# Activation and weight buffers 32 bytes further apart in SBUF

## The chip, the cores and the metric

The kernel runs on one core of a Trainium2 chip. The metric is the device time of one execution in microseconds (us). The kernel before took 1582.41 us as the median of three runs (1581.74 to 1587.0 us).

## The reference

Two layers of a transformer-like trunk run over 256 context tokens and 256 latent tokens of width 1024, batch 1, all in float32. Cut to the parts that matter here:

```
for i in range(2):
    mod, modc = silu(c) @ w_mod[i] + b_mod[i], silu(c_ctx) @ w_mod[i] + b_mod[i]
    h  = rms_norm(x,  norm1_g[i]) * (1 + mod[1])  + mod[0]
    hc = rms_norm(xc, norm1_g[i]) * (1 + modc[1]) + modc[0]
    parts = split(h @ w_in[i]), split(hc @ w_in[i])     # spatial-gating MLP, attention, Mamba-2
    x  = x + mod[2] * (concat(gmlp, attention, ssd) @ w_out[i])
    hf = rms_norm(x, norm2_g[i]) * (1 + mod[4]) + mod[3]
    # layer 0: one SwiGLU of width 2816 for all 512 tokens
    # layer 1: top 2 of 8 SwiGLU experts for the 256 latent tokens
    x  = x + mod[5] * f
```

The three head groups (a chunked spatial-gating MLP, windowed attention with a sink, a two-way Mamba-2 scan) lie between the input and the output projection; the change does not touch them.

## The kernel before

Everything lies transposed: the 1024 features are 8 blocks of 128 partitions, the 512 tokens run along a partition's bytes. `phase_a` computes layer 0 and the mixer of layer 1, `experts` the eight experts of layer 1.

**Weights.** Every weight is fetched as a piece of 128 partitions by 2048 floats (1024 KB, 8192 bytes in each partition) into a tile `wraw` (`Weights._load`; the DMA is issued by SyncE, L240). `wraw` tiles are slots of a ring: four in the pool `w`, and for the experts five more in the pool `mk` and three in the pool `mp`. `advance` fetches whenever a slot is free, and with twelve slots it runs far ahead in the expert stage.

**Two-term float32.** Most projections run as three matmuls in the type float32r. A weight piece is split by `Weights._split` into `whi` (a copy by ScalarE, L275) and `wlo` = `wraw` − `whi` (by VectorE, L276), each in two halves; the normed activations are split in `norm` into `ahi` (L520) and `alo` (L523 or L525), sixteen tiles `act` of 128 by 512. `project` then adds `ahi`·`whi`, `alo`·`whi` and `ahi`·`wlo` for each block of 128 features (all matmuls are recorded at L374, the line of the helper `mm`). In `project` the weight slice is the stationary operand and the activation tile the moving one. In `gmlp_v`, which writes `gvp`, it is the other way round: 128 tokens of `ahi` are stationary, and 264 columns of the weight tile move, from column 264·k in step k. Small experts multiply straight from `wraw` in plain float32.

**Order.** What stands in which order on an engine comes from the program's generators and from `Order`, a clock of estimated costs; no size or address of a tile enters it. SyncE's queue holds the weight DMAs in the order of the plan; a fetch waits for the last reader of the tile that had the slot.

**Where tiles lie.** A pool's tiles stand one after the other in each partition, and the pools one after the other. In the built program every one of the large tiles begins 224 bytes into a 256-byte row of SBUF (its start address modulo 256 is 224): `wraw`, `whi`, `wlo`, `ahi`, `alo`, the general tiles `g` (which hold `mhi`, `mlo`, `xT` and most others), and the slots of `mk` and `mp`. The reason is that each of these tiles has a multiple of 256 bytes (8448 or 8192 for weights, 2048 for the others). The one large tile that begins elsewhere is the second of the two `xp` tiles of the convolution, at 0 (a tile of 2080 bytes); the first is at 224.

Of the kernel before, what the change touches and what calls it, by code (L numbers as in the profile page):

```python
# [9 lines left out]
F32 = mybir.dt.float32  # L10
F32R = mybir.dt.float32r
# [7 lines left out]
P = 128  # L19
# [12 lines left out]
CONV_K = 5  # L32
GD = 264
WW = KB * GD

CONSTS = {}
NCONST = 0
# [172 lines left out]
def until(cond):  # L210
    while not cond():
        yield 0.5


class Weights:
# [14 lines left out]
    def _load(self):  # L230
        i = self.i_load
        _, src, width, _ = self.items[i]
        net = self.net
        if isinstance(src, tuple):
            _, p, c, j = src
            src = net.d["moe"][0, c, j] if p == NE - 1 else net.d["moe"][bass.ds(net.expert(p), 1), c, j].rearrange("e p f -> p (e f)")
        pool, bufs = self.ring[self.at_ring]
        self.at_ring = (self.at_ring + 1) % len(self.ring)
        t = pool.tile([P, WW if pool is net.wp else 2048], F32, tag="raw", name="wraw", bufs=bufs)
        net.nc.sync.dma_start(t[:, :width], src)  # L240
        self.raw[i] = t
        self.at[i] = net.o.clk
        self.queue = self.land[i] = max(self.queue + net.PIECE, net.o.clk + net.LANDS)
        self.raw_live += 1
        self.i_load += 1
# [7 lines left out]
    def _split(self, halves=2):  # L253
        i = self.i_split
        _, _, width, split = self.items[i]
        if not split:
            self.i_split += 1
            return
        net = self.net
        nc = net.nc  # L260
        t = self.raw[i]
        if not self.half:
            n = self.nsplit % self.nhi
            self.nsplit += 1
            pool, bufs = (net.wp, 2) if n < 2 else (net.mp, self.nhi - 2)
            ww = WW if pool is net.wp else 2048
            hi = pool.tile([P, ww], F32R, tag="hi", name="whi", bufs=bufs)
            lo = pool.tile([P, ww], F32R, tag="lo", name="wlo", bufs=bufs)
            self.hl[i] = (hi, lo, t) if split > 1 else (hi, lo)
            self.hi_live += 1  # L270
        hi, lo = self.hl[i][:2]
        n = net.NS
        for h in range(self.half, min(n, self.half + halves)):
            cs = slice(width // n * h, width // n * (h + 1))
            nc.scalar.activation(hi[:, cs], t[:, cs], AF.Copy)  # L275
            nc.vector.tensor_tensor(lo[:, cs], t[:, cs], hi[:, cs].bitcast(F32), op=ALU.subtract)  # L276
            self.splits = max(self.splits, net.o.clk, self.land[i]) + net.SPLIT
            self.ready.setdefault(i, self.splits + net.SPLIT)
        self.half += halves
        if self.half < n:  # L280
            return
        self.half = 0
        self.i_split += 1
        if split == 1:
            self.raw_live -= 1
            del self.raw[i]
# [54 lines left out]
class Net:  # L341
# [136 lines left out]
    def norm(self, l, which, xready, halves=False):  # L478

        nc = self.nc  # L480
        ps = self.pp.tile([P, 512], F32, tag="n", name="ssq", bufs=1)
        self.act = None

        def sums(k, a, b):

            sq0, sq = self.G(name="sq"), self.G(name="sq")
            nc.scalar.activation(sq0[:, a:b], self.xT[k - 1][:, a:b], AF.Square)
            nc.vector.tensor_tensor(sq[:, a:b], self.xT[k][:, a:b], self.xT[k][:, a:b], op=ALU.mult)
            nc.gpsimd.tensor_tensor(sq0[:, a:b], sq0[:, a:b], sq[:, a:b], op=ALU.add)
            return sq0  # L490

        last = KB - 2 if halves else KB
        for k in range(last):
            yield from until(lambda: all((k, s) in xready for s in range(2)))
            if k % 2:
                sq = sums(k, 0, T)
                if halves:
                    if k > 1:
                        nc.gpsimd.tensor_tensor(sq, sq, tot, op=ALU.add)
                    tot = sq  # L500
                else:
                    yield 2.5
                    self.mm(ps, self.c("ones"), sq, k == 1, k == KB - 1)
        a = 24 * which
        m = self.modT[l]
        sc = None
        mods_in = lambda: all((l, j) in self.mods_done for j in range(6 * which, 6 * which + 4))
        his, los = [], []
        for k in range(KB):
            his.append(self.gb.tile([P, 512], F32R, tag="act", name="ahi"))  # L510
            los.append(self.gb.tile([P, 512], F32R, tag="act", name="alo"))

        def apply(ks, s, r):
            cs = slice(256 * s, 256 * s + 256)
            for k in ks:
                u = self.G(name="nu")
                nc.vector.scalar_tensor_tensor(u[:, cs], self.xT[k][:, cs], sc[:, k, s:s + 1], r, op0=ALU.mult, op1=ALU.mult)
                sh = m[:, a + k, s:s + 1]
                hi, lo = his[k][:, cs], los[k][:, cs]
                nc.scalar.activation(hi, u[:, cs], AF.Identity, bias=sh)  # L520
                if k % 2:
                    nc.scalar.activation(u[:, cs], u[:, cs], AF.Identity, bias=sh)
                    nc.gpsimd.tensor_tensor(lo, u[:, cs], hi.bitcast(F32), op=ALU.subtract)  # L523
                else:
                    nc.vector.scalar_tensor_tensor(lo, u[:, cs], sh, hi.bitcast(F32), op0=ALU.add, op1=ALU.subtract)  # L525

        if halves:
            for s in (1, 0):
                yield from until(lambda: all((k, s) in xready for k in (KB - 2, KB - 1)))
                c0 = 256 * s  # L530
                sq = sums(KB - 1, c0, c0 + 256)
                if s == 1:
                    yield 1.8
                    self.mm(ps[:, c0:c0 + 256], self.c("ones"), tot[:, c0:c0 + 256], True, False)
                    self.mm(ps[:, c0:c0 + 256], self.c("ones"), sq[:, c0:c0 + 256], False, True)
                    r1 = self.rsqrt(ps[:, c0:c0 + 256], 1.0 / D, 256)[:, :256]
                    if mods_in():
                        sc = self.scales(l, which)
            if sc is None:
                yield from until(mods_in)  # L540
                sc = self.scales(l, which)
            apply(range(self.H1), 1, r1)
            yield 0.5
            self.mm(ps[:, :256], self.c("ones"), tot[:, :256], True, False)
            self.mm(ps[:, :256], self.c("ones"), sq[:, :256], False, True)
            r0 = self.rsqrt(ps[:, :256], 1.0 / D, 256)[:, :256]
            apply(range(self.H1, KB), 1, r1)
            apply(range(KB), 0, r0)
            yield self.H2
            self.act = (his, los)  # L550
            return
        r = self.rsqrt(ps, 1.0 / D, T)
        yield from until(mods_in)
        sc = self.scales(l, which)
        for k in range(KB):
            for s in range(2):
                apply((k,), s, r[:, 256 * s:256 * s + 256])
        yield 6.0
        self.act = (his, los)
# [644 lines left out]
    def plan(self):  # L1204
# [6 lines left out]
        def win(l):  # L1211
            n = self.mods_seq()[1] + self.MODS_C if l else 4
            for x in self.ORDER[l]:
# [3 lines left out]
                elif x == "g":  # L1217
                    it.append((("wgd", l), d["wgd"][l], WW, True))
                else:
# [583 lines left out]
    def overflow_of(self, e, past=0):  # L1803
# [28 lines left out]
        for c in range(NCH):  # L1832
            w = []
            for i in range(3):
                t_ = self.wp.tile([P, WW], F32, tag="raw", name="wraw", bufs=self.nraw)
                nc.sync.dma_start(t_[:, 0:2048], self.d["moe"][e, c, i].rearrange("e p f -> p (e f)"))
                w.append(t_)
            ps = self.bank("ogu")
# [106 lines left out]
```

## Time and profile before

| | |
|---|---|
| median of three runs | 1582.41 us |
| the profiled execution | 1583.83 us |
| its span, first to last instruction | 1582.1 us |
| mean granted TensorE clock | 0.978 |
| PE busy | 1500.2 us (95%) |
| DVE busy | 821.2 us (52%) |
| ACT busy | 666.7 us (42%) |
| DMA queue 1 | 392.03 MB, 62.2% of 16 engines' span |

PE is TensorE's matmuls, PEld its weight loads, DVE VectorE, ACT ScalarE, POOL GpSimd, SP SyncE. The span has two stages: up to about 890 us the phase before the experts, with DMA engines busy a third of the time; from about 900 us to 1545 us the experts, where the DMA engines are busy nearly without a break. A matmul's start is recorded; its end is modelled, so the distance from start to start of successive matmuls tells their rate better than the length shown.

### The profile page before, as it was taken

Reading aid. Unit: us, or ns where it says so; the run is one execution under the profiler, and the core shown is the slowest. Engines: PE = TensorE matmul, PEld = TensorE weight load, DVE = VectorE, ACT = ScalarE, POOL = GpSimd, SP = SyncE. Lnnn points to the kernel's source line nnn. Section 1 sums busy time; section 2 is a strip of 40 time slices with the busy share of each in tenths; the row PEclk is TensorE's granted clock in tenths of the full one; section 3 lists DMA queues with packets and bytes.
Section 4 is the critical chain, followed back from the end, with each engine's and each line's share of the span. In section 5 each row is a group of like instructions: output and inputs, shape, how many; then the busy total and the mean of one; then the engine's idle time right before and its main releaser. Section 6 shows DMA issues by size and latency. Waiting matters only on the chain. (4 is left out here: it accounts for less than half of the span.)

```text
span 1582.1 us, 23498 instructions
## 1 busy us (share of the span) xinstructions
PE 1500.2 (95%) x9302; PEld 1081.1 (68%) x9303; DVE 821.2 (52%) x1481; ACT 666.7 (42%) x1189; POOL 102.6 (6%) x135
## 2 busy tenths in 40 slices
PE   5999998899999999999999899999999999999997
PEld 1766675787887787878757776666566666656654
DVE  2687568543232333378774344544465444654545
ACT  3566644443222312266455354444343443433441
POOL 1200123210000000030300000000000000000000
PEclk9999999999999999999999899999999999999998
DMA  9422055333323323333164499999998999999994
GB/s 372 152 106 107 28 211 202 133 133 112 129 91 149 133 107 113 112 141 142 56 267 181 152 418 419 419 419 420 418 390 358 371 413 417 419 402 407 419 420 158
DMA packets 57715, 396.10 MB, mean 250 GB/s; under 512 B 6528, under 2 KB 8576, under 8 KB 10496
## 3 DMA queue, kind: packets, MB, share of 16 engines
q1 hardware_dynamic: 56016, 392.03, 62.2%
q10 hardware_dynamic: 1584, 2.52, 0.4%
q8 instruction: 75, 1.23, 0.3%
q14 instruction: 40, 0.33, 0.1%
HBM read 393.47 MB, written 1.05 MB: 249 GB/s over the span
## 5 line engine op out<-in xcount | busy, mean ns | idle before, releaser
L276 DVE TENSOR_TENSOR wlo<-wraw,whi 128x1024 fp32r<-128x1024 f32 (+2 forms) x318 | 377.0, 1222 | 161.2 <-ACT whi L275 155.9
L275 ACT ACTIVATE whi<-wraw 128x1024 fp32r<-128x1024 f32 (+2 forms) x318 | 320.0, 1047 | 148.5 <-PE fd L374 57.9
L374 PE MATMUL gu<-whi,xw 128*128 128x512 f32 x528 | 169.1, 401 | 4.2 <-ACT whi L275 4.2
L374 PE MATMUL gu<-wraw,xs 128*64 128x256 f32 (+1 forms) x1760 | 166.2, 386 | 0.5 <-ACT xs L1484 0.5
L374 PEld LDWEIGHTS gu<-wraw,xs 128*64 128x64 f32 (+1 forms) x1760 | 94.4, 127 | 64.3 <-issue 14.6
L374 PEld LDWEIGHTS gu<-whi,xw 128*128 128x128 f32 x528 | 96.9, 190 | 24.5 <-ACT whi L275 6.1
L374 PE MATMUL gu<-wlo,xw 128*128 128x512 f32 x264 | 104.9, 397 | 3.5 <-DVE wlo L276 3.5
L1162 DVE TENSOR_TENSOR fsil<-fsil,fu 128x512 f32<-128x512 f32 x22 | 15.1, 688 | 153.5 <-PE fu L374 118.2
L374 PE MATMUL pys<-wraw,silx 128*32 128x256 f32 (+1 forms) x616 | 87.6, 480 | 6.8 <-DVE y L1770 4.1
L425 ACT ACTIVATE fsil<-fg 128x512 f32<-128x512 f32 x22 | 13.1, 598 | 174.3 <-PE fg L374 174.3
L1573 ACT ACTIVATE mid<-gu 128x256 f32<-128x256 f32 x55 | 21.0, 382 | 137.1 <-PE gu L374 137.1
L374 PE MATMUL fg<-ahi,whi 128*128 128x512 f32 (+1 forms) x192 | 72.3, 377 | 0.0
L374 PE MATMUL fg<-alo,whi 128*128 128x512 f32 (+1 forms) x192 | 71.6, 373 | 0.2 <-POOL alo L523 0.2
L374 PE MATMUL fg<-ahi,wlo 128*128 128x512 f32 (+1 forms) x192 | 71.4, 372 | 0.0
L374 PE MATMUL fu<-alo,whi 128*128 128x512 f32 (+1 forms) x192 | 71.4, 372 | 0.0
L374 PE MATMUL fu<-ahi,wlo 128*128 128x512 f32 (+1 forms) x192 | 71.3, 372 | 0.0
L374 PE MATMUL fu<-ahi,whi 128*128 128x512 f32 (+1 forms) x192 | 71.3, 372 | 0.0
L374 PE MATMUL fd<-mhi,whi 128*128 128x512 f32 (+1 forms) x188 | 70.7, 376 | 0.0
L374 PE MATMUL fd<-mlo,whi 128*128 128x512 f32 (+1 forms) x188 | 70.6, 375 | 0.0
L374 PE MATMUL fd<-mhi,wlo 128*128 128x512 f32 (+1 forms) x188 | 70.6, 375 | 0.0
L374 PE MATMUL modp<-wraw,csil 128*32 128x512 f32 x384 | 56.7, 628 | 12.0 <-ACT csil L425 6.9
L374 PEld LDWEIGHTS gu<-wlo,xw 128*128 128x128 f32 x264 | 49.9, 189 | 18.3 <-DVE wlo L276 7.4
(342 smaller groups left out, 2831.8 us busy)
## 6 DMA issues: line engine op xcount, KB each, us to landing
wraw<-in_moe_dram SPq DMA_DIRECT2D x264, 1024.0 KB, 12.6
wraw<-in_wmod_dram SPq DMA_DIRECT2D x48, 1024.0 KB, 6.4
wraw<-in_fgu_dram SPq DMA_DIRECT2D x22, 1024.0 KB, 4.8
wraw<-in_win_dram SPq DMA_DIRECT2D x16, 1024.0 KB, 4.9
wraw<-in_wout_dram SPq DMA_DIRECT2D x8, 1024.0 KB, 6.2
wraw<-in_fdn_dram SPq DMA_DIRECT2D x8, 1024.0 KB, 6.2
wraw<-in_fdn_dram SPq DMA_DIRECT2D x4, 768.0 KB, 4.9
wraw<-in_wgd_dram SPq DMA_DIRECT2D x2, 1056.0 KB, 4.9
```

Source lines behind the costliest of these rows:

```text
L275: nc.scalar.activation(hi[:, cs], t[:, cs], AF.Copy)
L276: nc.vector.tensor_tensor(lo[:, cs], t[:, cs], hi[:, cs].bitcast(F32), op=ALU.subtract)
L374: self.nc.tensor.matmul(out, l, r, start=start, stop=stop)
L425: self.last_act = self.nc.scalar.activation(out, in_, func, **kw)
L1162: self.nc.vector.tensor_tensor(s, s, pu, op=ALU.mult)
L1573: self.nc.scalar.activation(v, ps[:, :256], AF.Copy)
```

## The change

Three widths grow by eight floats, 32 bytes: tiles `wraw`, `whi` and `wlo` of the pool `w` (2112 to 2120 columns) and the `act` tiles (512 to 520, of which 512 are used). Nothing else is edited.

```diff
+SKEW = 8
@@ Weights._load
-        t = pool.tile([P, WW if pool is net.wp else 2048], F32, tag="raw", name="wraw", bufs=bufs)
+        t = pool.tile([P, WW + SKEW if pool is net.wp else 2048], F32, tag="raw", name="wraw", bufs=bufs)
@@ Weights._split
-            ww = WW if pool is net.wp else 2048
+            ww = WW + SKEW if pool is net.wp else 2048
             hi = pool.tile([P, ww], F32R, tag="hi", name="whi", bufs=bufs)
             lo = pool.tile([P, ww], F32R, tag="lo", name="wlo", bufs=bufs)
@@ norm
-            his.append(self.gb.tile([P, 512], F32R, tag="act", name="ahi"))
-            los.append(self.gb.tile([P, 512], F32R, tag="act", name="alo"))
+            his.append(self.gb.tile([P, 512 + SKEW], F32R, tag="act", name="ahi")[:, :512])
+            los.append(self.gb.tile([P, 512 + SKEW], F32R, tag="act", name="alo")[:, :512])
@@ overflow_of
-                t_ = self.wp.tile([P, WW], F32, tag="raw", name="wraw", bufs=self.nraw)
+                t_ = self.wp.tile([P, WW + SKEW], F32, tag="raw", name="wraw", bufs=self.nraw)
```

In the built program the start addresses modulo 256 become:

| tiles | before | after |
|---|---|---|
| `wraw`, four slots in `w` | 224 each | 224, 0, 32, 64 |
| `whi`, two tiles | 224 each | 96, 128 |
| `wlo`, two tiles | 224 each | 160, 192 |
| `act`, sixteen tiles | 224 each | 224, 0, 32, 64, 96, 128, 160, 192, twice over |
| `wraw`, five slots in `mk`, three in `mp` | 224 each | 224 each |
| `g` tiles, `xw`, `mh`, `ml`, `hr` | 224 each | 224 each |
| `xp`, two tiles | 224, 0 | 224, 0 |

The eight tiles of `w` grow by 8 · 32 = 256 bytes together, so all that stands behind them moves by one whole row and keeps its place within one. The instructions of every engine, their order, and the semaphores and values they wait for are the same in the two built programs; only addresses differ.

## Rows read from the trace of the kernel before

**Rows 1.** Page, head and part 1: busy us (share of span) xinstructions.

```profile
span 1582.1 us, 23498 instructions
...
PE 1500.2 (95%) x9302; PEld 1081.1 (68%) x9303; DVE 821.2 (52%) x1481; ACT 666.7 (42%) x1189; POOL 102.6 (6%) x135
```

**Rows 2.** Engines by stretch; its first line names the columns.

```profile
core 0: us, PE busy (x) PEld busy (x) DVE busy (x) ACT busy (x) POOL busy (x), PEclk, DMA share, GB/s
...
250.00:500.00 250.00, 242.05 (x1240) 198.45 (x1239) 110.64 (x162) 77.42 (x115) 21.22 (x18) 1.00 0.35 128
500.00:665.00 165.00, 165.00 (x747) 133.79 (x746) 55.73 (x75) 41.83 (x54) 1.29 (x1) 1.00 0.32 115
...
920.00:1100.00 180.00, 174.87 (x1156) 117.98 (x1157) 86.21 (x106) 83.83 (x136) 0.00 (x0) 0.99 1.01 419
...
1300.00:1500.00 200.00, 192.84 (x1302) 125.03 (x1301) 106.90 (x143) 84.06 (x129) 0.00 (x0) 0.98 1.01 413
```

**Rows 3.** DMA in 920 to 1100 us: queue, packets, MB, share; issues, us to landing.

```profile
q1 hardware_dynamic: 10333, 75.24, 100.9%
...
wraw<-in_moe_dram SPq DMA_DIRECT2D x74, 1024.0 KB, 16.0
```

**Rows 4.** PE in time, 512 columns, 560 to 566 us: start, length.

```profile
559.64 0.39 PE L374 MATMUL fd<-mlo,whi 128*128 128x512 f32 x1
...
565.99 0.39 PE L374 MATMUL fd<-mhi,wlo 128*128 128x512 f32 x1
```

**Rows 5.** PE in time, 256 columns, 300 to 303 us.

```profile
299.73 0.28 PE L374 MATMUL op<-ahi,wlo 128*128 128x256 f32 x1
...
300.81 0.28 PE L374 MATMUL op<-ahi,wlo 128*128 128x256 f32 x1
```

**Rows 6.** PE in time, `gvp`, 264 columns: every third matmul of 24 in a row.

```profile
717.53 0.28 PE L374 MATMUL gvp<-whi,ahi 128*128 128x264 f32 x1
...
717.89 0.29 PE L374 MATMUL gvp<-whi,ahi 128*128 128x264 f32 x1
...
718.26 0.28 PE L374 MATMUL gvp<-whi,ahi 128*128 128x264 f32 x1
...
718.62 0.28 PE L374 MATMUL gvp<-whi,ahi 128*128 128x264 f32 x1
...
718.98 0.29 PE L374 MATMUL gvp<-whi,ahi 128*128 128x264 f32 x1
...
719.35 0.28 PE L374 MATMUL gvp<-whi,ahi 128*128 128x264 f32 x1
...
719.70 0.28 PE L374 MATMUL gvp<-whi,ahi 128*128 128x264 f32 x1
...
720.06 0.28 PE L374 MATMUL gvp<-whi,ahi 128*128 128x264 f32 x1
...
720.43 0.28 PE L374 MATMUL gvp<-whi,ahi 128*128 128x264 f32 x1
```

**Rows 7.** Groups by line and shape: xcount | busy us, mean ns | idle before.

```profile
L276 DVE TENSOR_TENSOR wlo<-wraw,whi 128x1024 fp32r<-128x1024 f32 x306 | 364.4, 1227 | 160.4 <-ACT whi L275 155.2 <-PE tok L379 4.2
...
L374 PE MATMUL gu<-whi,xw 128*128 128x512 f32 x528 | 169.1, 401 | 4.2 <-ACT whi L275 4.2
...
L374 PE MATMUL fd<-mhi,whi 128*128 128x512 f32 x164 | 63.8, 389 | 0.0
...
L374 PE MATMUL fg<-alo,whi 128*128 128x512 f32 x160 | 62.4, 390 | 0.0
```

**Rows 8.** Page, part 5: VectorE at 512 elements.

```profile
L1162 DVE TENSOR_TENSOR fsil<-fsil,fu 128x512 f32<-128x512 f32 x22 | 15.1, 688 | 153.5 <-PE fu L374 118.2
```

**Rows 9.** Single lines, ns min/median/max: L276 at 94-100 us, L275 at 704-709 us, L783 everywhere.

```profile
L276 DVE TENSOR_TENSOR wlo<-wraw,whi x2: 1249/1250/1251, 96.6 to 97.9; 128x1056 fp32r<-128x1056 f32 x2
...
L275 ACT ACTIVATE whi<-wraw x2: 1071/1071/1071, 704.5 to 705.9; 128x1056 fp32r<-128x1056 f32 x2
...
L783 DVE SCALAR_TENSOR_TENSOR convacc<-xp,params,convacc x48: 479/740/752, 85.3 to 747.7; 128x512 f32<-128x512 f32 x40, 128x256 f32<-128x256 f32 x8
```

## The prediction

> **What bounds the kernel now.** The page's head and first part come first: PE is busy for 1500.2 of 1582.1 us [rows 1], but a share over the whole span hides that the kernel has two stages with different limits. The view by stretches parts them [rows 2]. From 500 to 665 us PE is busy for 165.00 of 165.00 us at granted clock 1.00, with the DMA share at 0.32: there every nanosecond that a matmul gains or loses is a nanosecond of the kernel. From 920 to 1100 us and from 1300 to 1500 us the DMA share is 1.01, at 419 and 413 GB/s. The DMA view of the first of these stretches says what this is: one queue's packets take 100.9% of the sixteen engines' time, and a fetch lands 16.0 us after its issue [rows 3]. One fetch of 1024 KB is 1.0486 MB, and at 419 GB/s it takes 2.50 us, so some six are always queued. In the expert stage the fetches set the pace, and PE, DVE and ACT only follow.
>
> So an address can matter in two ways: through the rate of PE's matmuls before 890 us, and through the rate of the fetches after it. VectorE and ScalarE are third: they limit where a split ends last before a matmul, which is seldom (4.2 us of idle PE before `gu` for `whi`, [rows 7]).
>
> **What the change does, part by part.** No instruction, DMA or wait is added, removed or moved; so nothing has to be hidden, and the sum consists of durations alone. Of the tiles only those listed as moved get another place within a 256-byte row: 4 of the 12 fetch slots have new widths and 3 of them a new place; `whi` and `wlo` of `w` all move; the `act` tiles spread over eight places. The `g` tiles, `xw` and eight fetch slots keep theirs.
>
> *Matmuls.* In `fd`, where three matmuls of 512 columns follow each other without a break, 28 intervals take 565.99 − 559.64 = 6.35 us, 226.8 ns each [rows 4]. [...] The direct test stands in the trace too. In `gvp` the moving weights of step k begin at column 264·k, 1056·k bytes, which is 32 bytes further in a row at each step, while the stationary `ahi` stays at 224 plus a multiple of 512 bytes. Three matmuls a step, eight steps, so all eight places occur. The starts are 0.36, 0.37, 0.36, 0.36, 0.37, 0.35, 0.36 and 0.37 us apart [rows 6]: 2.90 us for 24, 120.8 ns each, no step out of line by more than the 10 ns of the reading. The step in which weights and activation share a place is neither quicker nor slower. The roles of the operands are swapped against `project`, which is why this is strong but no proof. I take 0 ns for each matmul. For the ends: none of the eight places can differ by more than about 0.01 us over three matmuls, 3.3 ns for each. In `project` a piece of weights meets 8 steps, 3 terms and 2 column blocks, 48 matmuls; with 22 pieces for `fg` and `fu` and 16 for the two input projections that makes 38 · 48 = 1824, some 1800 of the 9302 PE instructions [rows 1], with both operands on moved tiles. 1800 · 3.3 ns is 5.9 us either way if every one went to one end; as the places spread over all eight, I keep half of it, ±3 us.
>
> *Splits on DVE and ACT.* L276 takes a mean of 1227 ns for 1024 elements, and the same kind of operation, there with one input in PSUM, takes 688 ns for 512 [rows 7, 8]: (1227 − 688)/512 = 1.05 ns for each further element. Two SBUF inputs at one place cost no visible extra over one. Again places already differ in the trace. The two halves of the gate piece are 1056 elements; the second begins 4224 bytes on, at place (224 + 4224) mod 256 = 96. DVE takes 1249 and 1251 ns for the two halves of one layer's piece, ACT 1071 and 1071 for the other layer's [rows 9]. The convolution reads `xp` at 224 and at 0 in turn, at four shifts each; forty operations on 512 elements and eight on 256 stay between 479 and 752 ns with a median of 740, and a second level for the second tile doesn't show [rows 9]. I take 0, with ±10 ns as the end. The 306 splits of 1024 elements at 10 ns are 3.1 us of DVE time, and DVE is busy for 55.73 of 165 us and 86.21 of 180 us [rows 2]; PE's own stream and the fetches cover them, so nothing reaches the end. Without that cover it would be the 3.1 us.
>
> *Fetches.* Here no row of mine compares two places, since every slot begins at 224; so the cost has to be bounded. Upper end: 0, the time of a fetch goes by its bytes. Lower end: it goes by the bytes from the start of the first row. A partition's 8192 bytes from place 224 span 8416 from the row's start; from 0, 32 and 64 they span 8192, 8224 and 8256, shorter by 2.7%, 2.3% and 1.9%. In the expert stage 264 fetches go round 12 slots, 22 for each, at 2.50 us. 22 · 2.50 · (0.027 + 0.023 + 0.019) = 3.8 us less. If it went by the number of rows touched (33 from 224, 32 from 0, 33 from 32 and 64), only one slot would gain, 22 · 2.50/33 = 1.7 us. A loss has no such source: no slot begins later in a row than before. In the first stage the DMA share of 0.32 to 0.35 hides any gain. I take 0: it is the value nearest to what the same layout gives today, 419 GB/s steadily.
>
> [...]
>
> The sum is 0 against the profiled execution's 1583.83 us (span 1582.1 and 1.7 around it). That execution lies 1.4 us above the median of the three runs, so the forecast is that median, 1582.4 us.
>
> **The rivals.** *A, fetches gain by their place*, the lower end above: 1582.4 − 3.8 = 1578.6 us, or 1580.7 if it goes by rows touched. For it: the expert stage is bound by fetches. Against it: only 3 of 12 slots move, and nothing in the trace shows a loss at 224. Both values lie within 0.3% (4.7 us), about what a measurement of this kernel can tell from no change.
>
> [...]
>
> *C, slower: operands at unlike places hinder each other*, which equal places avoid today because the streams run in step. [...] The price is taken from `gu<-whi,xw`, the slowest of the 512-column groups, 401 against 389 ns [rows 7], though fetches and waits may explain it: 1800 · 12 ns · 7/8 = 18.9 us, 1601.3 us. It decides as soon as a matmul costs over 4.7 us/1800 = 2.6 ns more. Against it: `gvp` again, where seven of eight pairs are unlike.
>
> *D, less is changed than it seems*: the eight tiles of `w` add up to 256 bytes, so most tiles stay where they were. This is so, whatever the places cost; it makes each of the others smaller and gives 1582.4.
>
> **How the numbers follow.** No change (with D) gets 0.80, A 0.11, B 0.05, C 0.04. A counts as within 0.3% but at its end it comes near the edge, so I give 0.02 of it to faster. Faster is 0.05 + 0.02 = 0.07; slower is C's 0.04 and 0.01 more for a run like the highest of the three; the same is what is left, 0.88. The range reaches down to A's end, 1578.5, and up to the highest of the three runs, 1587.0; it leaves out B and C.
>
> **What would show it.** In the profile after, the intervals of `fd` should again be 227 ns and those of `op` 120; the mean of `fg<-alo,whi` should stay at 390 ns and that of `fd` at 389; L276 at 1227 ns within 10; PE busy in 500 to 665 us without a gap; the DMA rate from 920 to 1100 us at 419 GB/s, within 3. [...] Any change of more than 5 us would make the prediction wrong, above all one before 890 us.

## The result

| | before | after |
|---|---|---|
| median | 1582.54 us (4 runs) | 1596.22 us (4 runs) |
| lowest to highest | 1581.74 to 1587.0 | 1593.57 to 1596.65 |
| profiled execution, its span | 1583.83, 1582.1 us | 1593.57, 1591.7 us |
| mean granted clock | 0.978 | 0.977 |

The changed kernel takes 1.0078 times as long, with an interval of 1.0061 to 1.0095: 12.3 us more (9.7 to 15.0). The forecast was no change, and the time lies outside its range. The profiled executions differ by 9.7 us, their spans by 9.6 us; where those lie can be read from the traces.

The page's head and first part, to set against [rows 1]: the same 23498 instructions, PE busy for 11.9 us longer, the span 9.6 us longer.

```profile
span 1591.7 us, 23498 instructions
...
PE 1512.1 (95%) x9302; PEld 1081.5 (68%) x9303; DVE 821.6 (52%) x1481; ACT 667.6 (42%) x1189; POOL 103.5 (7%) x135
```

Next three stretches, with the columns and the windows of [rows 2].

```profile
500.00:665.00 165.00, 165.00 (x732) 131.10 (x731) 52.25 (x70) 39.88 (x51) 0.00 (x0) 1.00 0.32 115
...
920.00:1100.00 180.00, 173.43 (x1158) 117.22 (x1157) 85.21 (x110) 85.05 (x142) 0.00 (x0) 0.99 1.01 420
1300.00:1500.00 200.00, 192.94 (x1284) 125.01 (x1285) 106.69 (x145) 84.22 (x130) 0.00 (x0) 0.98 1.00 413
```

From 500 to 665 us PE is busy without a gap at granted clock 1.00, as before, but starts 732 matmuls in the 165 us instead of 747 [rows 2]. Nothing waits more; each matmul takes longer (747/732 = 1.020). The DMA rate from 920 to 1100 us is 420 GB/s against 419. The matmuls in time show the price of one:

```profile
565.12 0.39 PE L375 MATMUL fd<-mlo,whi 128*128 128x512 f32 x1
...
571.59 0.39 PE L375 MATMUL fd<-mhi,wlo 128*128 128x512 f32 x1
...
299.07 0.28 PE L375 MATMUL op<-ahi,wlo 128*128 128x256 f32 x1
...
300.12 0.28 PE L375 MATMUL op<-ahi,wlo 128*128 128x256 f32 x1
...
724.50 0.28 PE L375 MATMUL gvp<-whi,ahi 128*128 128x264 f32 x1
...
727.42 0.28 PE L375 MATMUL gvp<-whi,ahi 128*128 128x264 f32 x1
```

The first column is the start. `fd`: 28 intervals in 6.47 us, 231.1 ns each, against 226.8 [rows 4]. `op` with 256 columns: nine in 1.05 us, 116.7 ns against 120.0 [rows 5]. `gvp` with 264: 24 in 2.92 us, 121.7 ns against 120.8 [rows 6]. So one edit makes matmuls of 512 columns slower, those of 256 columns faster, and leaves the mean of those of 264 nearly as it was. The groups by line and shape agree, and the other engines' lines stay:

```profile
L277 DVE TENSOR_TENSOR wlo<-wraw,whi 128x1024 fp32r<-128x1024 f32 x306 | 364.4, 1228 | 160.9 <-ACT whi L276 154.9 <-PE tok L380 4.4
...
L375 PE MATMUL gu<-whi,xw 128*128 128x512 f32 x528 | 171.1, 405 | 4.2 <-ACT whi L276 4.2
...
L375 PE MATMUL fd<-mhi,whi 128*128 128x512 f32 x164 | 64.9, 396 | 0.0
...
L375 PE MATMUL fg<-alo,whi 128*128 128x512 f32 x160 | 62.9, 393 | 0.0
```

Against [rows 7], `gu`, `fd` and `fg` gain 3 to 7 ns in length, the split on VectorE 1 ns.

**Where the 9.6 us lie.** First and last starts of three tiles mark the stages. Here before and then after; a row has the number, the length in ns (least/median/most) and the first and last start in us.

```profile
L374 PE MATMUL fg<-ahi,whi x192: 279/389/504, 309.1 to 649.1; 128*128 128x512 f32 x160, 128*128 128x256 f32 x32
...
L374 PE MATMUL fd<-mhi,whi x188: 277/389/390, 414.1 to 684.3; 128*128 128x512 f32 x164, 128*128 128x256 f32 x24
...
L374 PE MATMUL gu<-whi,xw x528: 387/389/775, 928.5 to 1534.3; 128*128 128x512 f32 x176
```

```profile
L375 PE MATMUL fg<-ahi,whi x192: 278/393/500, 308.8 to 655.7; 128*128 128x512 f32 x160, 128*128 128x256 f32 x32
...
L375 PE MATMUL fd<-mhi,whi x188: 274/394/404, 415.9 to 691.3; 128*128 128x512 f32 x164, 128*128 128x256 f32 x24
...
L375 PE MATMUL gu<-whi,xw x528: 387/394/775, 934.2 to 1543.8; 128*128 128x512 f32 x176
```

The SwiGLU of layer 0, first `fg` to last `fd`, takes 684.3 − 309.1 = 375.2 us before and 691.3 − 308.8 = 382.5 us after: +7.3. The experts, first `gu` to last `gu`, take 605.8 and 609.6 us: +3.8. What lies ahead of the first comes to −0.3 us, what lies between the two (244.2 and 242.9 us, the mixer of layer 1 with its many 256-column matmuls) to −1.3 us, and the tail to +0.1. 7.3 + 3.8 − 0.3 − 1.3 + 0.1 = 9.6. The lengths of the SwiGLU and of the experts, called the SwiGLU stretch and the expert stretch, are given for the experiments too. Only these two differences are clear of what varies between executions: before and in the experiments that keep the operands alike in the stretch in question (3, 5, 9, 10 and 12), the SwiGLU stretch is 375.2 to 376.6 us and the expert stretch 604.9 to 605.8, while what lies between the two is 240.8 to 244.8, so the −1.3 us there shows nothing.

### The profile page after: what moved, and what is told of

Its sections match the earlier page's. It is cut to its first block, busy times and chain, and to the rows that moved or that the text cites. A ratio compares the mean times of both kernels' runs of the same rounds, so it can differ in the third digit from the quotient of the medians.

```text
span 1591.7 us, 23498 instructions
## 1 busy us (share of the span) xinstructions
PE 1512.1 (95%) x9302; PEld 1081.5 (68%) x9303; DVE 821.6 (52%) x1481; ACT 667.6 (42%) x1189; POOL 103.5 (7%) x135
## 3 DMA queue, kind: packets, MB, share of 16 engines
HBM read 393.47 MB, written 1.05 MB: 248 GB/s over the span
## 5 line engine op out<-in xcount | busy, mean ns | idle before, releaser
L276 ACT ACTIVATE whi<-wraw 128x1024 fp32r<-128x1024 f32 (+2 forms) x318 | 320.3, 1048 | 152.2 <-PE fd L375 59.3
```

## The experiments

**How a matmul is read.** For each kernel I took the mean distance from a float32r matmul's start to the next one's where the next follows without a wait (distances of 220 to 245 ns for 512 columns, 100 to 135 ns for 256), by the tile of the first of the two. It is worked out from all such starts in the trace, in ns:

| | fd 512 | fg 512 | gu 512 | py 512 | fg 256 | op 256 |
|---|---|---|---|---|---|---|
| before | 226.7 | 227.4 | 228.9 | 227.9 | 120.0 | 119.5 |
| after | 232.1 | 231.5 | 232.7 | 232.4 | 118.3 | 117.7 |
| 1 weights' pool alone | 232.0 | 232.4 | 232.7 | 232.4 | 120.1 | 117.9 |
| 2 `act` tiles alone | 226.8 | 231.1 | 228.9 | 227.7 | 117.7 | 119.5 |
| 3 all at byte 0 | 226.7 | 227.4 | 228.2 | 227.6 | 120.0 | 119.6 |
| 4 weights' pool at 96 | 233.3 | 234.7 | 232.4 | 233.0 | 120.0 | 118.7 |
| 5 fetch tiles alone | 226.7 | 227.4 | 228.8 | 227.8 | 120.0 | 119.5 |
| 6 `wlo` alone at 96 | 231.1 | 231.2 | 232.8 | 231.4 | 119.1 | 119.1 |
| 7 `act` 16 bytes on | 227.0 | 231.7 | 228.9 | 227.7 | 113.4 | 119.5 |
| 8 `act` 64 bytes on | 226.7 | 229.2 | 228.8 | 227.9 | 117.7 | 119.5 |
| 9 `mp` tiles alone | 226.7 | 227.4 | 232.5 | 232.8 | 119.9 | 119.5 |
| 10 `act` 256 bytes wider | 226.7 | 227.4 | 228.8 | 227.7 | 119.9 | 119.5 |
| 11 `act` 4 bytes on | 226.7 | 236.4 | 228.8 | 227.7 | 123.5 | 119.4 |
| 12 `act` 16 on in layer 1 | 226.7 | 227.4 | 228.8 | 227.7 | 120.0 | 119.5 |

Behind the arrow of a line stands the moving operand first, then the stationary one. In `fd` `mhi` or `mlo` moves, in `fg` and `op` `ahi` or `alo`, and `whi` or `wlo` is stationary. In `gu` and `py` it is the other way round, as in `gvp`: `whi` or `wlo` moves, and `xw`, `mh` or `ml` is stationary. "At 224" and the like mean the start address modulo 256, and two operands are alike when these are equal.

**1. The weights' pool alone.** The two lines on `act` are undone, so that they stay at 224.

```
-    his.append(self.gb.tile([P, 512 + SKEW], F32R, tag="act", name="ahi")[:, :512])
-    los.append(self.gb.tile([P, 512 + SKEW], F32R, tag="act", name="alo")[:, :512])
+    his.append(self.gb.tile([P, 512], F32R, tag="act", name="ahi"))
+    los.append(self.gb.tile([P, 512], F32R, tag="act", name="alo"))
```

> Only the tiles of the pool w (wraw, whi, wlo) get the 32 bytes; act stays at 224. Theory 1 (relation): a matmul of 512 columns takes 227 ns from start to start when its moving operand and the weights loaded beside it begin at the same place of a 256-byte row, and some 232 ns when they don't. Then fd, fg, fu and gu all read about 232, the 256-column matmuls about 118 instead of 120, and the time is that of the changed kernel, 10 to 14 us above before. Theory 2 (absolute place): 224 is a good place and every other is bad, whatever the partner's; here it expects the same. Theory 3 (the activation tiles make the loss, because 16 of the 24 moved tiles are theirs): fg, fu, fd, gu at 227, no loss.

Measured: 1597.29 us, ratio 1.0092 (1.0067 to 1.0117) against 1584.0 us before in the same runs. The SwiGLU stretch is 693.5 − 311.1 = 382.4 us and the expert stretch 609.7: all of both losses. Of the 256-column matmuls `op` came to 117.9 ns as expected, while `fg` stayed at 120.1.

```profile
L375 PE MATMUL fd<-mhi,whi x188: 274/394/404, 417.7 to 693.5; 128*128 128x512 f32 x164, 128*128 128x256 f32 x24
...
L375 PE MATMUL gu<-whi,xw x528: 387/395/775, 936.8 to 1546.5; 128*128 128x512 f32 x176
```

**2. The `act` tiles alone.** The diff's two lines on `act`, all else as before.

```
-    his.append(self.gb.tile([P, 512], F32R, tag="act", name="ahi"))
-    los.append(self.gb.tile([P, 512], F32R, tag="act", name="alo"))
+    his.append(self.gb.tile([P, 512 + SKEW], F32R, tag="act", name="ahi")[:, :512])
+    los.append(self.gb.tile([P, 512 + SKEW], F32R, tag="act", name="alo")[:, :512])
```

> Only the 16 act tiles get the 32 bytes; all tiles of w stay at 224. Theory 1: fg, fu and the input projections of layer 0 at about 232 ns (seven of eight pairs unlike), fd, gu and py unchanged at 227 to 229. Loss 1152 + about 380 matmuls times 4.5 ns, less about 1 us that the 256-column matmuls of layer 1 win: 5 to 6 us, 1588. Theory 2: the same in fg and fu, if the moving operand's place counts; if only the weights' place counts, no loss at all. Theory 3: the whole loss, 10 to 14 us.

Measured: 1587.14 us, ratio 1.0024 (1.0011 to 1.0037). The SwiGLU stretch grows by 5.1 us to 380.3, all of it in `fg` and `fu`; `fd`, which reads no `act` tile, keeps 226.8 ns, and the expert stretch 605.8 us.

```profile
L375 PE MATMUL fg<-ahi,whi x192: 277/392/501, 311.5 to 656.5; 128*128 128x512 f32 x160, 128*128 128x256 f32 x32
...
L375 PE MATMUL fd<-mhi,whi x188: 278/389/398, 418.6 to 691.8; 128*128 128x512 f32 x164, 128*128 128x256 f32 x24
...
L375 PE MATMUL gu<-whi,xw x528: 387/389/715, 936.9 to 1542.7; 128*128 128x512 f32 x176
```

Either side may be moved (`fg` has 232.4 ns in 1 and 231.1 here, against 227.4), and only matmuls that read a moved tile change: `gu` keeps 228.9 ns here. 1 and 2 don't add up to the change: once the weights lie elsewhere the pairs are unlike already, and moving `act` too adds nothing (the SwiGLU stretch is 382.4 us in 1 and 382.5 after).

**3. All at byte 0.** A pad of 32 bytes ahead of the pools puts the large tiles of five pools, with 7 of the 12 fetch slots, at 0 together.

```
+    keep.tile([P, 8], F32, name="pad")
```

> No tile is widened; 32 bytes are put ahead of the pools w, g, keepA, act and mp, so that all their tiles begin at 0 instead of 224 (the five slots in mk, acc and hr stay at 224, xp at 0 and 32). Theory 1: partners are again at one place, so 227 ns for 512 columns and 120 for 256, and the time of before, 1582.5 within 3 us. Theory 2: 224 was the good place, so 231 or more everywhere and a loss of 10 us or more; or, if an aligned start is the best one, a gain. If fetches go by their first row (rival A), the expert stage gains up to 7 slots of 12 times 2.7% of 2.5 us times 22, 10 us.

Measured: 1583.53 us, ratio 0.9992 (0.9977 to 1.0007). Intervals as before, the expert stretch 605.4 us.

```profile
L374 PE MATMUL fd<-mhi,whi x188: 278/389/389, 416.0 to 686.3; 128*128 128x512 f32 x164, 128*128 128x256 f32 x24
...
L374 PE MATMUL gu<-whi,xw x528: 387/389/775, 931.0 to 1536.4; 128*128 128x512 f32 x176
```

The place itself costs the matmuls nothing, 224 or 0 (`fd` 226.7 ns at both): it is the difference between two operands. The fetches do become faster. The rate by 40 slices of the span, before and then here, shows it where the queue is full; from the 25th to the 29th slice (949 to 1147 us before) it is 418 to 420 GB/s before and 424 to 426 here:

```profile
GB/s 372 152 106 107 28 211 202 133 133 112 129 91 149 133 107 113 112 141 142 56 267 181 152 418 419 419 419 420 418 390 358 371 413 417 419 402 407 419 420 158
...
GB/s 376 147 106 107 28 213 195 137 133 96 144 83 156 133 107 113 103 138 153 58 268 181 159 395 424 426 426 425 425 358 359 376 409 418 425 389 414 426 425 146
```

That is 1.4% more, and the expert stretch is no shorter for it (605.4 against 605.8 us).

**4. The weights' pool at 96, all alike.** Two pads of 128 bytes around the pool's first tiles: every weight tile at 96, the activations at 224.

```
+    if self.nsplit == 1:
+        net.wp.tile([P, 32], F32, tag="pad1", name="pad1", bufs=1)
 ...
+    self.wp.tile([P, 32], F32, tag="pad0", name="pad0", bufs=1)
     self.w = Weights(self, self.plan(), self.nraw, self.nhi)
```

> All tiles of w begin at 96 (128 bytes further), each other tile at 224 as before: among themselves whi and wlo are alike, against act, g and xw unlike by half a row. Theory 1: unlike partners, so 231 to 232 ns in fd, fg and gu, and 10 to 14 us above before. If instead it is the mixture of places among the weights that costs (whi at 96 and 128, wlo at 160 and 192 in the changed kernel), then 227 and no loss.

Measured: 1597.45 us, ratio 1.0091 (1.0067 to 1.0116); SwiGLU stretch 385.2 us, +10.0, expert stretch 609.7. That weights differ among each other isn't needed; one fixed distance of 128 bytes costs as much as the change's spread, in the SwiGLU more. In time the steps alternate, some 229 and some 238 ns. It goes by turns and not by the term: in `fd`, with three terms to a step of the sum, the 492 distances alternate without exception, and each term has 82 near 229 and 82 near 238. With the six terms of `fg` and `fu` two of the three long ones always fall to `fg`, whose mean of 234.7 is high for that reason alone (`fu` has 231.9):

```profile
335.10 0.40 PE L376 MATMUL fg<-ahi,whi 128*128 128x512 f32 x1
335.34 0.39 PE L376 MATMUL fg<-alo,whi 128*128 128x512 f32 x1
335.56 0.40 PE L376 MATMUL fg<-ahi,wlo 128*128 128x512 f32 x1
335.80 0.39 PE L376 MATMUL fu<-ahi,whi 128*128 128x512 f32 x1
...
337.90 0.40 PE L376 MATMUL fg<-ahi,whi 128*128 128x512 f32 x1
```

**5. The fetch tiles alone.** The four `wraw` of the weights' pool at 224, 0, 32 and 64 as in the change, a pad that puts `whi` and `wlo` back to 224.

```
+    t = pool.tile([P, WW + SKEW if pool is net.wp else 2048], F32, tag="raw", name="wraw", bufs=bufs)
 ...
+    if self.nsplit == 1:
+        net.wp.tile([P, 32], F32, tag="pad0", name="pad0", bufs=1)
```

> Only the four wraw slots of the pool w get the 32 bytes (224, 0, 32, 64); whi, wlo, act and the rest stay at 224, by 128 bytes put between wraw and whi. Theory 1 (relation between the two operands of a float32r matmul): no such matmul reads wraw, so fd, fg, fu and gu stay at 227 to 229 ns and the time is that of before within 2 us; the splits (L275, L276) and fetches, whose places now differ from those of whi and wlo, cost nothing. A rival that puts part of the loss on splits or fetches expects L276 or L275 longer, or the expert stage slower, by up to 4 us in all.

Measured: 1584.32 us against 1583.73, ratio 1.0006 (0.9991 to 1.002); SwiGLU stretch 375.2 us, expert stretch 604.9. Neither the fetches nor the splits, which read these tiles, carry any of the loss.

**6. `wlo` alone at 96.** Pads of 128 bytes around the `lo` tiles.

```
     hi = pool.tile([P, ww], F32R, tag="hi", name="whi", bufs=bufs)
+    if self.nsplit == 1:
+        net.wp.tile([P, 32], F32, tag="pad0", name="pad0", bufs=1)
     lo = pool.tile([P, ww], F32R, tag="lo", name="wlo", bufs=bufs)
+    if self.nsplit == 1:
+        net.wp.tile([P, 32], F32, tag="pad1", name="pad1", bufs=1)
```

> Only the two wlo tiles move, to 96, half a row from the rest. In fd the order is mhi-whi, mlo-whi, mhi-wlo, so one matmul has weights unlike its own stream, and another loads unlike weights for the next. If what counts is the weights loaded beside the stream, mlo-whi (while wlo is loaded) becomes longer, mhi-wlo (while whi is loaded) stays at 227 ns; if it is a matmul's own pair, mhi-wlo becomes longer and mlo-whi stays. The sum over the three is some 4 to 13 ns above 680 either way. With no effect at all, 227 in all three.

Measured, in one run: 1591.07 us. It was to tell whether a matmul is hindered by its own weights' place or by that of the weights loaded beside it for the next one. By term, in the table's way: `mhi`·`whi`, all alike, 226.7 ns; `mlo`·`whi`, own pair alike and `wlo` loaded beside it, 232.5; `mhi`·`wlo`, own pair unlike and `whi` loaded beside it, 234.2. Either theory expected one long step; there are two. So this either/or has the wrong form: an unlike pair lengthens the step on both sides of it. The groups show it in lengths:

```profile
L378 PE MATMUL fd<-mhi,wlo 128*128 128x512 f32 x164 | 65.1, 397 | 0.0
L378 PE MATMUL fd<-mlo,whi 128*128 128x512 f32 x164 | 64.9, 396 | 0.0
...
L378 PE MATMUL fd<-mhi,whi 128*128 128x512 f32 x164 | 63.8, 389 | 0.0
```

**7, 8, 10 and 11. How far apart.** The `act` tiles are 64 floats wider, so that all stay at one place, and are used from float `n` on: 4 floats (16 bytes), 16 (64 bytes), 0 (only a row further apart) and 1 (4 bytes).

```
+    his.append(self.gb.tile([P, 576], F32R, tag="act", name="ahi")[:, n:n + 512])
+    los.append(self.gb.tile([P, 576], F32R, tag="act", name="alo")[:, n:n + 512])
```

> All act tiles begin 16 bytes further in the row than everything else (at 240; the tiles are 2304 bytes wide, so that they stay alike among themselves). Theory 1 with rows of 256 bytes read as a whole: 16 bytes are 4 of 64 columns, partners are out of step by that, and fg and fu read above 229 ns, fd and gu 227 to 229. If places are told apart only by 32 or 64 bytes, fg and fu stay at 227.

> All act tiles begin 64 bytes further in the row than everything else (at 32 of the next row), all alike. Theory 1: fg and fu at 230 to 235 ns, the 256-column matmuls of layer 1 that read act (qp, xbcp, zp, gup) below 119, fd, gu and op as before. If the mixture of places within act is what costs in the changed kernel, fg and fu stay at 227.

> The act tiles are 2304 bytes wide, so they lie 256 bytes further apart, and each begins at 224 as before. Theory 1 (only the place in the row counts): fg and fu at 227 ns, no loss. If distance itself counts, fg and fu above 229.

> The act tiles begin 4 bytes further in the row than all else (at 228), one column of a float. If what counts is a match to the byte, fg and fu read about 231 as with 16 bytes; if places are told apart by 16 bytes, they stay at 227.

Measured, in one run each: 1591.15, 1582.7, 1582.34 and 1593.51 us. By `fg`, 512 columns: 231.7 ns at 16 bytes, 229.2 at 64, 227.4 with the wider tiles and no shift, 236.4 at 4. Experiment 10 clears the tiles' distance: whole rows more are free, within 0.1 ns. 64 bytes were expected to give 230 to 235 and 4 bytes some 231; both are misses, and the cost isn't one size for any unlike place. The 256 columns go their own way: 113.4 ns at 16 bytes, 117.7 at 64, 123.5 at 4. The four times say little by themselves, since 23 runs of the kernel before, in the series of experiments 10 and 11, lie between 1578.77 and 1588.44 us; the reading rests on the intervals. Experiment 11 in time, then the same place before:

```profile
336.11 0.41 PE L374 MATMUL fg<-ahi,whi 128*128 128x512 f32 x1
...
337.29 0.40 PE L374 MATMUL fu<-ahi,wlo 128*128 128x512 f32 x1
```

```profile
334.11 0.39 PE L374 MATMUL fg<-ahi,whi 128*128 128x512 f32 x1
...
335.24 0.39 PE L374 MATMUL fu<-ahi,wlo 128*128 128x512 f32 x1
```

Five intervals are 1.18 us, 236 ns each, against 1.13 us, 226 ns. And experiment 7 at 256 columns, 114 intervals in 12.92 us, 113.3 ns each:

```profile
318.04 0.28 PE L374 MATMUL fu<-ahi,whi 128*128 128x256 f32 x1
...
330.96 0.28 PE L374 MATMUL fu<-ahi,whi 128*128 128x256 f32 x1
```

**9. The experts' tiles alone.** A pad of 128 bytes at the start of pool `mp` moves `xw`, `mh`, `ml` and its three fetch slots to 96; the weights and all of layer 0 stay.

```
+    self.mp.tile([P, 32], F32, name="pad", bufs=1)
```

> Only the tiles of the pool mp move (xw, mh, ml, three wraw slots, the small tiles), all to 96, while whi and wlo stay at 224; everything before the experts is as before. Theory 1: up to 900 us no difference; in the expert stage gu and py (weights moving, activations loaded) read 232 to 233 ns instead of 228 to 229. If the experts' matmuls decide when a wraw slot comes free, the stage becomes 3 to 5 us longer, as it did when the tiles of w moved; if the fetches alone set its pace, as the prediction read it, the time stays within 1 us of before.

Measured: 1587.44 us against 1583.69, ratio 1.0020 (1.0008 to 1.0033). `gu` goes to 232.5 ns, `py` to 232.8; the expert stretch is 1538.5 − 928.8 = 609.7 us, 3.9 more, and the SwiGLU has `fg` at 227.4 ns:

```profile
L374 PE MATMUL fg<-ahi,whi x192: 283/389/562, 309.8 to 651.1; 128*128 128x512 f32 x160, 128*128 128x256 f32 x32
...
L374 PE MATMUL gu<-whi,xw x528: 387/393/775, 928.8 to 1538.5; 128*128 128x512 f32 x176
```

So the expert stage, in which the DMA share is 0.96 to 1.01 from 920 to 1500 us, still pays for slower matmuls. In experiment 1 the same 3.9 us came from the weights' side with these tiles at 224.

**12. The 256-column gain, where it may pay.** `act` starts 16 bytes further on in layer 1 alone, where most matmuls that read it have 256 columns.

```
+    n0 = 4 if l == 1 else 0
+    his.append(self.gb.tile([P, 576], F32R, tag="act", name="ahi")[:, n0:n0 + 512])
+    los.append(self.gb.tile([P, 576], F32R, tag="act", name="alo")[:, n0:n0 + 512])
```

> A try at a version better than before: the act tiles begin at 224 in layer 0 and 16 bytes further in layer 1, whose projections mostly have 256 columns (qp, zp, gup, most of xbcp), which were shorter when unlike. Theory 1 with the intervals seen at 16 bytes: some 330 matmuls of 256 columns win about 2.5 ns, 96 of 512 lose 4: 0.4 us less, below what times can tell; layer 0 and the experts as before.

Measured: 1581.63 us against 1583.69, ratio 0.9990 (0.9976 to 1.0004): not to be told from no change. The matmuls of layer 1 did what was expected (`gup` with 256 columns 115.7 ns against 119.8, `xbcp` 117.4 against 119.6; `kp` with 512 columns 231.6 against 228.5), but they are too few. No version tried is faster than before beyond its interval.

## Why the prediction was wrong

**The step that failed is the one on matmuls, "I take 0 ns for each matmul".** In this kernel a float32r matmul of 512 columns takes some 4 to 5 ns more when its moving and its stationary operand begin at unlike places of a 256-byte row, as the change spreads them (`fd` 232.1 against 226.7 ns, `gu` 232.7 against 228.9).

`gvp`, "the direct test", held the effect, and the reading was too coarse for it. Its pairs lie at all eight distances before the change already, so its mean could hardly move (120.8 and 121.7 ns), and its steps were read three terms at a time, to 10 ns. Taken to the nanosecond from the starts in the trace before, the 23 single distances within a group of 24 matmuls, each as the median of the eight groups, run from 116 to 129 ns, and the longest is the first of step k = 7. Experiment 4 moves the weights by 128 bytes, which is four steps of 32 bytes: there the same pattern comes four steps earlier, with the 129 ns at the first of step 3 (correlation with the 23 before: 0.97). In experiments 3, 5, 9 and 10, which leave these two operands as far apart as before, it stands where it stood (0.93 to 0.95). I had seen the weak point in the swapped roles. That was not it: in `gu` and `py` the weights move as in `gvp`, and both lose at 512 columns (228.9 to 232.7 and 227.9 to 232.4 ns). The number of columns, with the roles of `project`, is enough to turn the sign (`fg` in experiment 7 against before: 231.7 against 227.4 ns for 512, 113.4 against 120.0 for 256). "None of the eight places can differ by more than … 3.3 ns" was a bound for the sum of three terms in `gvp` and was used for `project`.

**The count was short too.** I counted 1824 matmuls "with both operands on moved tiles". Experiments 1 and 2 show that one moved operand is enough. That takes in `fd`, 492 matmuls of 512 columns, and the experts' `gu` and `py`, 792 + 396, the ones with the weights moving. The sum as it should have been, from the intervals above: `fd` 492 · 5.4 = 2.7 us, `fg` and `fu` 960 · 4.4 = 4.2 us, together 6.9 for the 7.3 us of the SwiGLU stretch; `gu` 792 · 3.8 and `py` 396 · 4.5, together 4.8, for the 3.8 us of the expert stretch; only some 700 and 300 of these follow the one ahead without a wait, and they alone come to 4.0.

**"In the expert stage the fetches set the pace, and PE, DVE and ACT only follow" is wrong as far as PE goes.** The row that shows it stood there: from 920 to 1100 us PE is busy for 174.87 of 180 us [rows 2], while the DMA share is 1.01. Two resources were near their limit, and I read the full queue as the pace. From 1100 to 1300 us the queue isn't even full, while PE is as busy:

```profile
1100.00:1300.00 200.00, 194.66 (x1489) 128.38 (x1487) 100.85 (x145) 83.74 (x141) 0.00 (x0) 0.99 0.96 390
```

Experiments 9 and 3 are the proof from both sides: matmuls some 4 ns longer (`gu` 3.6, `py` 4.9) make the stage 3.9 us longer, and fetches at 424 to 426 instead of 418 to 420 GB/s make it no shorter.

**Rival C was right as to what the time goes by.** "Operands at unlike places hinder each other" came with 0.04, and unlike places do cost time at 512 columns (`fd` 226.7 to 232.1 ns); that equal places avoid it "because the streams run in step" no run shows. Its price of 12 ns was guessed from the slow mean of `gu`, which has other causes (`gu` has 401 ns in [rows 7] with like places); its 18.9 us had too much per matmul and too few matmuls. Its turning point, 2.6 ns a matmul, was right: the matmuls went past it.

**Rival B, that operands at one place collide and unlike places save time, is refuted at 512 columns**, since by the mean of a tile matmuls at like places (before, experiments 3 and 10; `fd` 226.7 ns in each) are the fastest that these runs show. The saving for each matmul behind its 0.05 was the author's estimate, and no run shows it: `fd`, `fg`, `gu` and `py` lost 3.8 to 5.4 ns. At 256 columns there is a gain (`op` 119.5 to 117.7 ns), too small to be told in the time: experiment 12 went after it and found no change.

**Splits at 0 were right; fetches at 0 were right by luck.** The split's mean is 1228 against 1227 ns, a gate piece's second half is no slower (1249 and 1251 ns, after as before), and experiment 5 moves all of the pool's fetch tiles without a change in time. The rate of the fetches, though, did change with where the slots begin, as rival A had it: with seven of twelve slots at the start of a row (experiment 3) a full queue moves 1.4% more (424 to 426 against 418 to 420 GB/s). The change puts one slot there, and its rate is 420 against 419 GB/s. No time came of it because the stage follows PE, which isn't the reason that the prediction gave. The prediction's lower end, 2.7% for a slot at 0, would make 7/12 of 2.7%, some 1.6%, an estimate from the slots' places alone; what in a fetch costs the difference, no run shows.

**What stays open.** The two profiled spans account for 9.6 us and the two stretches for 11.1, while the timed ratio says 12.3 (9.7 to 15.0); what the rest is, these two executions don't tell. Why unlike places cost time isn't settled. The trace tells that the load of the stationary operand keeps its length (`gu<-whi,xw` on PEld has 190 ns before and 191 after) and runs beside the matmul ahead of it (from 500 to 665 us PE is busy for all of the 165.00 us and PEld for 131.10 after), that an unlike pair lengthens the steps on both sides (232.5 and 234.2 against 226.7 ns in experiment 6), that the changed kernel's matmuls take 231 to 233 ns even where the next stationary operand shares the moving one's place, and that the cost depends on the distance without a plain order: 236.4 ns at 4 bytes, 231.7 at 16, 229.2 at 64, and at 128 bytes 229 and 238 by turns. Nor is it a matter of the pair alone: in experiment 8, where all pairs of `fg` lie 64 bytes apart, the step from `alo`·`whi` has 230.3 ns and that from `ahi`·`wlo` 227.4. What the runs show is that the two operands' places matter to each other: at 512 columns `fd` has 226.7 ns alike and 232.1 as the change spreads them, and at 256 the sign turns.

## What to carry to other kernels

Let the moving and the stationary operand of back-to-back float32r matmuls of 512 columns begin at the same byte of a 256-byte row, and pad tiles by whole multiples of 256 bytes: that was free here (`fg` 227.4 ns in experiment 10 as before), while 32 bytes on the weights' pool cost 0.9% (experiment 1). When a test in the trace before is to stand for another instruction, take one of the same size, and read it as finely as the effect is large: three distances of `gvp` at a time, to 10 ns, hid single ones of 116 to 129 ns. And a full DMA queue doesn't make a stage fetch-bound while PE is busy for 97% of it: here matmuls some 4 ns slower lengthened it by 3.9 us (experiment 9), and fetches 1.4% faster didn't shorten it (605.4 against 605.8 us, experiment 3).

## What was not expected of the hardware

- Start to start of 512-column float32r matmuls: 226.7 to 228.9 ns with operands at the same place of a 256-byte row, by tile 229 to 236 ns at the other distances tried; 4 bytes apart is the worst (236.4), 64 bytes the mildest (229.2), and at 128 bytes the steps are 229 and 238 ns by turns.
- At 256 columns the sign turns: in `fg` 120.0 ns alike, 113.4 at 16 bytes, 117.7 at 64, but 120.0 at 128 and 123.5 at 4. At 264 columns, with all eight distances among the pairs, single distances in `gvp` run from 116 to 129 ns, and their mean is 121 to 122 before and after.
- The place itself doesn't matter: all at 224 and all at 0 give the same intervals to 0.1 ns in `fd` (226.7), `fg` (227.4) and `op` (119.5 and 119.6).
- Fetches with 8192 bytes in each partition: 418 to 420 GB/s at a full queue with all twelve slots 224 bytes into a row, 424 to 426 with seven of them at its start (experiment 3).
